# Turning the heads' outputs in 32x32 blocks on VectorE instead of transposing them on TensorE

## The chip, the core and the metric

The kernel runs on one core of one Trainium2 chip. The core has five engines, each with its own instruction queue: TensorE (PE, matrix products into PSUM), VectorE (DVE), ScalarE (ACT), GpSimd (POOL) and SyncE (SP, which here only issues DMA transfers); POOL and ACT issue DMA transfers too. Queues run in order and wait for each other by semaphores. The metric is the device time of one execution in microseconds (us).

## The reference: what is computed

One layer of a decoder trunk over 1024 tokens and 16 meta tokens ahead of them, 1024 channels, in float32. Two recurrent branches run side by side, each with four heads of 256 output channels: GLA and mLSTM. Each head's output is normalized over its 256 channels, scaled by a gain per channel, and multiplied by a gate; the branches are projected, merged and added, and a gated convolutional FFN follows.

```python
o_gla = from_chunks(head_rms(o_gla, gla_norm)) * silu(g_r)
o_ml  = from_chunks(head_rms(o_ml, ml_norm))   * sigmoid(m_o)
y = sigmoid(gate_a) * (o_gla @ w_branch_gla) + sigmoid(gate_b) * (o_ml @ w_branch_ml)
h = h + y @ w_out
def head_rms(y, g):
    return y * rsqrt(mean(y * y, axis=-1) + EPS) * g
```

The change concerns the way of a head's output from the recurrence, where tokens are rows, to the product with its gate, where channels are rows.

## The kernel before

**Stages.** The eight heads come first (s = 0 to 3 GLA, s = 4 to 7 mLSTM), then gates, branch products, merge and FFN. Matrix products that need float32 are done as three products of high and low parts. A scheduler places the instructions on each engine; the program's order is the default, and `tc.issue_after(x)` keeps a block behind the instruction x.

**Heads.** `main(gen)` steps through the dense projections (`value_proj`, `key_query_proj`, TensorE's bulk) and, at each step, lets one step of the recurrence of the head in work (`side`) and one of a finished head's epilogue (`closing`) in between. So head s is closed while head s+1 is scored and the projections for later heads run. In a GLA head, scores are made of `pk` tiles (decayed keys and queries, products on DVE and POOL, exponentials on ACT), TensorE's score products (`sc`, L862, PSUM tag "s"), and a masked copy into `A` (L879, DVE).

**The epilogue `post`.** A head's output lies in `oraw[0]` and `oraw[1]`, each 128 tokens x (4 chunks x 256 channels), and `om`, 2 rows that hold the last two meta tokens. ACT scales its rows by the reciprocal norm (L735, L736). Then, for each half j of the head's 256 channels: eight TensorE transposes of 128x128 (L744) turn the half to channels x tokens in two PSUM tiles `ot`; ACT copies each out into `of`, with the channel's gain as the scale (L746); a small transpose turns the meta rows (L757), which DVE copies out (L758); and one store by SP (L759) writes the 128 x 1026 half to the DRAM tile `osc`.

**Gates.** Gates are computed in pairs; the first eight pairs (q = 0 to 7) belong to the head halves, four pairs of GLA (`otdg`) and four of mLSTM (`otdm`). A pair's gates are computed by one Strassen-like scheme with four PSUM banks V, X, Y, Z per half of the tokens (`piece`), evicted by ACT and DVE (L1229 to L1245); weights are split on ACT and DVE (`gate_weights`, L1266 to L1293). `gate_finish(q - 1)` runs one pair behind: per gate it issues a load of the head half (`go`, two buffers "o0" and "o1") on POOL's queue (L1352), applies the gate's activation on ACT (L1353), multiplies on DVE into `go` (L1354), and stores the product from POOL's queue into `otd` (L1355). Loads stand in POOL's queue behind the stores of the pair before. The activated gates `gu` have two buffers of tag "u0", one of "u1", and for the last pairs every second one lies in "o1".

Of the kernel before, what the change touches and what calls it, by code (L numbers as in the profile page):

```python
# [9 lines left out]
F32 = mybir.dt.float32  # L10
# [7 lines left out]
P = 128  # L18
D = 1024
NM = 16  # L20
SEQ = 1024
# [24 lines left out]
def hybrid_kernel(ctx, tc, x, meta, norm_mix, w_in, b_in, gla_w_gate, gla_b_gate, gla_norm,  # L46
# [67 lines left out]
    with tc.issue_after(sent.ins):  # L114
        nc.scalar.activation(warm, one1, AF.Exp)

    rooted, flipped = [], {}

    def rstd_of(ss, n, w, pool, name):

# [384 lines left out]
    def cc(i):  # L505
        return col[:, i:i + 1]
# [28 lines left out]
            nc.vector.tensor_copy(lmask[b], mfs[:, P * (i + 1):P * (i + 2)])  # L535


    osc = {g: dram.tile([NK, P, NP], F32, name=f"osc{g}") for g in "gm"}
    gsc = {g: dram.tile([NK, P, NP], F32, name=f"gsc{g}") for g in "ab"}
    rsc = dram.tile([2, H, T], F32, name="rsc")  # L540
    msc = dram.tile([2 * H, T], F32, name="msc")
# [109 lines left out]
    def half_sums(t, m, c):  # L651
        for o, a, b in ((0, 1, 0), (1, 3, 1), (3, 3, 0), (2, 2, 3)):
            nc.gpsimd.tensor_tensor(t[:, o], t[:, a], t[:, b], OP.subtract)  # L653
        for i in range(2):
            nc.gpsimd.dma_start(tdn[i][m][:, :, 256 * c:256 * c + 256], t[:, 2 * i:2 * i + 2])
# [67 lines left out]
        yield  # L723


    def post(s, o, om, sc, ncols):

        h = s % 4
        g = "g" if s < 4 else "m"
        after = rooted[0]  # L730
        if 4 <= s < 7:
            with tc.issue_after(after.ins):
                after = token_sums(s - 3, nc.gpsimd)
        for c in range(NC):
            nc.scalar.activation(o(c), o(c), AF.Copy, scale=sc[:, c + 1:c + 2])  # L735
        nc.scalar.activation(om, om, AF.Copy, scale=sc[:2, 0:1])  # L736
        for _ in range(3 if s != 3 else 6):
            yield
        for j in range(2):
            of = hd.tile([P, T], F32, name=f"of{s}_{j}", tag="r", bufs=2)  # L740
            for gi in range(2):
                tp = ps.tile([P, 4, P], F32, name=f"ot{s}_{j}_{gi}", tag="s", bufs=3)
                for i in range(4):
                    nc.tensor.transpose(tp[:, i, :], o(4 * gi + i)[:, j * P:(j + 1) * P], ident)  # L744
                a, b = 2 + 512 * gi, 2 + 512 * (gi + 1)
                flipped[s] = nc.scalar.activation(of[:, a:b], tp.rearrange("p n w -> p (n w)"), AF.Copy,  # L746
                                                  scale=ncols[j]).ins
                if gi == 0:
                    yield
                    if 3 <= s < 7:  # L750
                        if j == 0:
                            with tc.issue_after(after.ins):
                                t = half_load(wp, "gst")
                        else:
                            half_sums(*t)
            tp = ps.tile([P, 4, P], F32, name=f"otm{s}_{j}", tag="s", bufs=3)
            nc.tensor.transpose(tp[:, 0, :2], om[:, j * P:(j + 1) * P], ident[:2, :2])  # L757
            nc.vector.tensor_scalar(of[:, 0:2], tp[:, 0, :2], ncols[j], None, OP.mult)  # L758
            nc.sync.dma_start(osc[g][2 * h + j], of[:, :NP])  # L759
            yield  # L760


# [46 lines left out]
    def gla(s):  # L809
# [74 lines left out]
        def level(b):  # L884


            if b == 1:
                p1 = raw.rearrange("p (n w) -> p n w", w=1)
                nc.scalar.activation(p1, lv(la[:, NM:], 1)[:, :, 1, :], AF.Exp, scale=1.0 / 16)
                nc.vector.tensor_tensor(p1, p1, lv(kv, 1)[:, :, 0, :], OP.mult)  # L890
                nc.vector.tensor_tensor(p1, p1, lv(qv, 1)[:, :, 1, :], OP.mult)
                return split_raw(f"pk{s}_1")
            pk = wtile(f"pk{s}_{b}")
            n = SEQ // (2 * b)
            pe, pl = (pk[:, 512 * i:512 * (i + 1)].rearrange("p (n w) -> p n w", w=b) for i in range(2))
            src = [lv(t, b)[:, :, 0, :] for t in (kv, bcv)]
            if b < 32:
                e = pk[:, :512].rearrange("p (i n h w) -> p i n h w", n=64 // b, h=2, w=b)
                pe = [e[:, :, :, 0, :], e[:, :, ::-1, 1, ::-1]]
                src = [[t.rearrange("p (i c n h w) -> p i c n h w", c=2, n=64 // b, h=2, w=b)[:, :, c, :, 0, :]  # L900
                        for c in range(2)] for t in (kv, bcv)]
            else:
                pe, src = [pe], [[t] for t in src]
            early = list(zip(pe, *src))
            b4 = lv(bcv, b)
            ref = b4[:, :, 0, b - 1:b].to_broadcast([P, n, b])
            for e, _, t in early:
                nc.vector.tensor_tensor(e, t[..., b - 1:b].to_broadcast(t.shape), t, OP.subtract)
            nc.vector.tensor_tensor(pl, b4[:, :, 1, :], ref, OP.subtract)
            with tc.issue_after(flipped[0]) if s == 1 and 0 in flipped else nullcontext():  # L910
                nc.scalar.activation(pk[:, :SEQ], pk[:, :SEQ], AF.Exp, scale=1.0 / 16)  # L911
            for eng, (e, k, _) in zip((nc.gpsimd, nc.vector), early):
                eng.tensor_tensor(e, e, k, OP.mult)  # L913
            nc.vector.tensor_tensor(pl, pl, lv(qv, b)[:, :, 1, :], OP.mult)
            return pk
# [117 lines left out]
        closing.append(post(s, o, om[:, :DV], sc, [cc(C_GN + j) for j in range(2)]))  # L1033


    above = []
# [1 line left out]
    def mlstm(s):  # L1038
# [119 lines left out]
        closing.append(post(s, o, om[:, :DV], sc, [cc(C_MN + 2 * h + j) for j in range(2)]))  # L1158


    def step(gens):
# [150 lines left out]
    def token_blocks():  # L1312
        for i in (0, 2, 1, 3):
            if i == 1:
                places()
            TB[i] = [gs.tile([P, 4, 514], F32R, name=f"T{p}{i}", tag=f"T{p}{i}") for p in "HL"]
        for p, c in enumerate((slice(0, W0), slice(W0, 514))):
            for i in (0, 2, 1, 3):
                nc.sync.dma_start(TB[i][1][:, :, c].bitcast(F32), tsc[p][i])
# [17 lines left out]
    def row(name, tag, bufs=1):  # L1337
        return gs.tile([P, T], F32, name=name, tag=tag, bufs=bufs)

    def places():  # L1340

        for i in range(2):
            go[0, i] = row(f"go0_{i}", f"o{i}")

    def gate_finish(q):
        for i, u in enumerate(gu.pop(q)):
            _, c, f, g, j = GATES[2 * q + i]
            if f is None:
# [3 lines left out]
            nc.gpsimd.dma_start(o[:, :NP], osc[g][j])  # L1352
            nc.scalar.activation(u[:, :NP], u[:, :NP], f, bias=cc(c))  # L1353
            nc.vector.tensor_tensor(o[:, :NP], u[:, :NP], o[:, :NP], OP.mult)  # L1354
            nc.gpsimd.dma_start(otd[g][j], o[:, :NP])  # L1355
# [779 lines left out]
```

## Time and profile before

| | |
|---|---|
| median of 3 runs | 1865.05 us (1864.66 to 1866.4) |
| profiled execution, from first to last instruction | 1865.1 us |
| TensorE's mean granted clock | 0.998 |
| busy: PE, DVE, ACT, POOL | 1846.0, 1227.9, 869.8, 427.5 us |
| transposes on TensorE (L744, L757) | 128 and 16, between 141 and 611 us of the span |
| gating products on DVE (L1354) | 16, between 661 and 803 us |

The profiled execution's own time is its span; it lies within the runs. The profile names instructions by line, engine, operation and tiles: `L744 PE MATMUL ot<-ident,or` is the transpose (a product with the identity) of a piece of `oraw` into `ot`. Durations of TensorE's instructions overlap, since matmuls are pipelined, so what one costs the queue is read from the distance between starts.

### The profile page before, as it was taken

The numbers are of one execution on the slowest core, as the hardware profiler recorded it, in microseconds if no ns is written. First come the engines' busy times: TensorE is split into PE (matmuls) and PEld (weight loads), VectorE is DVE, ScalarE is ACT, GpSimd is POOL, SyncE is SP. The second block draws the span as 40 slices with busy tenths as digits, with TensorE's granted clock in tenths as the row PEclk, the third lists the DMA queues.
The fourth block names the chain that finished last, engine by engine and source line by source line (L and its number), as shares of the span: only waits on it lengthen the run. The fifth ranks groups of instructions, "written<-read, shape, count | busy, mean of one in ns | idle before, by whom it ended". The sixth has DMA issues, their size and how long they took to land. (4 is left out here: it accounts for less than half of the span.)

```text
span 1865.1 us, 32629 instructions
## 1 busy us (share of the span) xinstructions
PE 1846.0 (99%) x13286; PEld 1768.5 (95%) x13286; DVE 1227.9 (66%) x1819; ACT 869.8 (47%) x1397; POOL 427.5 (23%) x485
## 2 busy tenths in 40 slices
PE   8999999999999999999999999999999999999998
PEld 7999999999999999999999999999999999977886
DVE  7966756655552566655523547798887887887876
ACT  6565564645544434322512335544434434465664
POOL 6310111205541001142381600012222222100100
PEclk9999999999999999999999999999999999999999
DMA  5211112144323655655963733333333333298894
GB/s 162 58 38 60 36 49 60 60 92 139 96 87 113 181 147 148 175 169 168 353 216 109 254 126 116 114 104 124 114 104 107 114 118 121 74 341 299 288 382 166
DMA packets 221820, 269.63 MB, mean 145 GB/s; under 512 B 13986, under 2 KB 177101, under 8 KB 221671
## 3 DMA queue, kind: packets, MB, share of 16 engines
q1 hardware_dynamic: 200447, 196.20, 34.0%
q0 software_dynamic: 18624, 62.62, 10.2%
q10 hardware_dynamic: 2600, 8.74, 1.3%
q8 instruction: 104, 1.70, 0.4%
q14 instruction: 45, 0.37, 0.1%
HBM read 197.91 MB, written 69.60 MB: 143 GB/s over the span
## 5 line engine op out<-in xcount | busy, mean ns | idle before, releaser
L653 POOL TENSOR_TENSOR ts<-ts 128x256 f32<-128x256 f32 x88 | 79.6, 911 | 47.0 <-DMA ts<-in_ffn_w_down_dram 44.9
L1654 POOL TENSOR_TENSOR SB<-SA,rg 128x512 f32<-128x512 f32 x20 | 32.4, 1622 | 240.2 <-issue 101.4
L276 PE MATMUL pv<-wH_mv,xH 128*128 128x256 f32 x256 | 74.8, 292 | 0.1
L276 PE MATMUL pv<-wH_gv,xH 128*128 128x256 f32 x256 | 74.5, 291 | 0.0
L1741 PE MATMUL po<-wH_wo,yH 128*128 128x256 f32 x256 | 72.5, 283 | 0.1
L276 PE MATMUL pv<-wH_gv,xL 128*128 128x256 f32 x256 | 72.0, 281 | 0.0
L276 PE MATMUL pv<-wL_mv,xH 128*128 128x256 f32 x256 | 71.9, 281 | 0.0
L1741 PE MATMUL po<-wL_wo,yH 128*128 128x256 f32 x256 | 71.7, 281 | 0.3 <-DVE wL_wo L147 0.3
L276 PE MATMUL pv<-wL_gv,xH 128*128 128x256 f32 x256 | 71.9, 281 | 0.0
L276 PE MATMUL pv<-wH_mv,xL 128*128 128x256 f32 x256 | 71.9, 281 | 0.0
L1741 PE MATMUL po<-wH_wo,yL 128*128 128x256 f32 x256 | 71.8, 281 | 0.0
L913 POOL TENSOR_TENSOR pk<-pk,kT 128x256 f32<-128x256 f32 (+1 forms) x24 | 29.6, 1237 | 182.7 <-ACT pk L911 165.1
L1689 DVE SCALAR_TENSOR_TENSOR cv<-u,fc,cv 128x1024 f32<-128x1024 f32 x44 | 65.1, 1482 | 0.4
L1636 POOL TENSOR_TENSOR A<-u2raw,A 128x512 fp32r<-128x512 f32 x20 | 42.4, 2122 | 86.3 <-ACT A L1635 86.3
L1447 PE MATMUL bg<-ogL,wH_bg 128*128 128x342 f32 x192 | 61.5, 320 | 0.0
L1447 PE MATMUL bg<-ogH,wH_bg 128*128 128x342 f32 x192 | 61.5, 320 | 0.0
L1447 PE MATMUL bm<-omH,wH_bm 128*128 128x342 f32 x192 | 61.4, 320 | 0.0
L1447 PE MATMUL bm<-omH,wL_bm 128*128 128x342 f32 x192 | 61.3, 319 | 0.0
L1447 PE MATMUL bg<-ogH,wL_bg 128*128 128x342 f32 x192 | 61.3, 319 | 0.0
L1447 PE MATMUL bm<-omL,wH_bm 128*128 128x342 f32 x192 | 61.2, 319 | 0.0
L280 DVE TENSOR_TENSOR v<-pv,bB 128x256 f32<-128x256 f32 x64 | 26.4, 417 | 39.5 <-PE pv L276 39.2
L1635 ACT ACTIVATE HA<-rg 128x1024 fp32r<-128x1024 f32 x16 | 17.0, 1060 | 73.0 <-PE Yu L1208 72.6
(821 smaller groups left out, 7511.3 us busy)
## 6 DMA issues: line engine op xcount, KB each, us to landing
gw<-in_w_in_dram SPq DMA_DIRECT2D x26, 512.0 KB, 5.7
ts<-in_ffn_w_down_dram POOLq DMA_DIRECT2D x44, 256.0 KB, 4.2
tdn<-ts POOLq DMA_DIRECT2D x44, 256.0 KB, 2.8
rg<-in_ffn_w_up_dram SPq DMA_DIRECT2D x22, 512.0 KB, 3.8
ru<-in_ffn_w_up_dram SPq DMA_DIRECT2D x22, 512.0 KB, 3.9
adr<-s SPq DMA_DIRECT2D x40, 256.0 KB, 2.8
rd<-in_ffn_w_down_dram SPq DMA_DIRECT2D x20, 512.0 KB, 11.2
do<-tdn SPq DMA_DIRECT2D x18, 512.0 KB, 6.0
```

Of the source, the lines that this page charges most:

```text
L276: nc.tensor.matmul(pt[:, :DV], a[:, k, t0:t0 + P], b[:, k % 4, :], start=(i == 0), stop=(i == 3 * NK - 1))
L280: nc.vector.tensor_tensor(vt[:n, c, :DV], pt[:n, :DV], bB[:n, :], OP.add)
L653: nc.gpsimd.tensor_tensor(t[:, o], t[:, a], t[:, b], OP.subtract)
L913: eng.tensor_tensor(e, e, k, OP.mult)
L1447: nc.tensor.matmul(pt[:, i, :n], a[:, k, :], b[k][:, base + t0:base + t0 + n], start=(k == 0 and j == 0), stop=(k == NK - 1 and j == 2))
L1635: nc.scalar.activation(h, src, AF.Copy)
L1636: eng.tensor_tensor(l, src, h.bitcast(F32), OP.subtract)
L1654: late.tensor_tensor(sb[:, 0:4], sa[:, 0:4], rg[:, 0:4], OP.subtract)
L1689: nc.vector.scalar_tensor_tensor(y, u[:, j:SEQ + j], fc[:, j, jj:jj + 1], y, OP.mult, OP.add)
L1741: nc.tensor.matmul(pt[:, :DV], a, b[:, k % 4, :], start=(k == 0 and i == 0), stop=(k == NK - 1 and i == len(terms) - 1))
```

## The change

`post` no longer uses TensorE. The meta rows are stored as they are to a DRAM tile `omd`. Per half of the tokens (j now counts halves of the tokens, `oraw[j]`) one DVE instruction turns 128x1024 in blocks of 32x32 (L745 in the new file): within each block, tokens and channels change places, and blocks are written in the order channel block, chunk. Four SP stores, one per 32 partitions, write 32 x 8 x 128 elements into `osc`, which now has 1024 columns, whose rows are channels and whose columns stand in the order (partition block a, chunk c, token j). ACT's evictions, the PSUM tiles `ot` and the ordering of one exponential behind the eviction (`flipped`) are gone.

The gating does the rest. `load_head(q, i)` loads the meta columns (128x2, from `omd` with rows and columns exchanged, L1340) and the 128x1024 main part (L1341) on POOL's queue into the only buffer left, "o0". The product becomes five scalar_tensor_tensor instructions on DVE, head x gain x gate, one for the meta columns (L1353) and four for the partition blocks (L1357), the gate read and written at the permuted places; the result stays in `gu` and is stored from there (L1358). The load of the pair's second head is issued after the first head's products, and that of the next pair's first head at the end of `gate_finish`. `gu` has two buffers of each kind.

```diff
@@ -535,7 +535,8 @@
-    osc = {g: dram.tile([NK, P, NP], F32, name=f"osc{g}") for g in "gm"}
+    osc = {g: dram.tile([NK, P, SEQ], F32, name=f"osc{g}") for g in "gm"}
+    omd = {g: dram.tile([H, 2, DV], F32, name=f"omd{g}") for g in "gm"}
     gsc = {g: dram.tile([NK, P, NP], F32, name=f"gsc{g}") for g in "ab"}
     rsc = dram.tile([2, H, T], F32, name="rsc")
     msc = dram.tile([2 * H, T], F32, name="msc")
@@ -723,7 +724,7 @@
         yield
 
 
-    def post(s, o, om, sc, ncols):
+    def post(s, oraw, om, sc):
 
         h = s % 4
         g = "g" if s < 4 else "m"
@@ -732,31 +733,27 @@
             with tc.issue_after(after.ins):
                 after = token_sums(s - 3, nc.gpsimd)
         for c in range(NC):
-            nc.scalar.activation(o(c), o(c), AF.Copy, scale=sc[:, c + 1:c + 2])
+            o = oraw[c // 4][:, DV * (c % 4):DV * (c % 4 + 1)]
+            nc.scalar.activation(o, o, AF.Copy, scale=sc[:, c + 1:c + 2])
         nc.scalar.activation(om, om, AF.Copy, scale=sc[:2, 0:1])
+        nc.sync.dma_start(omd[g][h], om)
         for _ in range(3 if s != 3 else 6):
             yield
+        dst = osc[g][2 * h:2 * h + 2].rearrange("t (q i) n -> i (t q) n", i=32)
         for j in range(2):
-            of = hd.tile([P, T], F32, name=f"of{s}_{j}", tag="r", bufs=2)
-            for gi in range(2):
-                tp = ps.tile([P, 4, P], F32, name=f"ot{s}_{j}_{gi}", tag="s", bufs=3)
-                for i in range(4):
-                    nc.tensor.transpose(tp[:, i, :], o(4 * gi + i)[:, j * P:(j + 1) * P], ident)
-                a, b = 2 + 512 * gi, 2 + 512 * (gi + 1)
-                flipped[s] = nc.scalar.activation(of[:, a:b], tp.rearrange("p n w -> p (n w)"), AF.Copy,
-                                                  scale=ncols[j]).ins
-                if gi == 0:
-                    yield
-                    if 3 <= s < 7:
-                        if j == 0:
-                            with tc.issue_after(after.ins):
-                                t = half_load(wp, "gst")
-                        else:
-                            half_sums(*t)
-            tp = ps.tile([P, 4, P], F32, name=f"otm{s}_{j}", tag="s", bufs=3)
-            nc.tensor.transpose(tp[:, 0, :2], om[:, j * P:(j + 1) * P], ident[:2, :2])
-            nc.vector.tensor_scalar(of[:, 0:2], tp[:, 0, :2], ncols[j], None, OP.mult)
-            nc.sync.dma_start(osc[g][2 * h + j], of[:, :NP])
+            t32 = hd.tile([P, T], F32, name=f"of{s}_{j}", tag="r", bufs=2)[:, :SEQ]
+            nc.vector.transpose(t32.rearrange("p (b c j) -> p c b j", b=8, c=4),
+                                oraw[j][:, :SEQ].rearrange("p (c b j) -> p c b j", c=4, b=8))
+            yield
+            if 3 <= s < 7:
+                if j == 0:
+                    with tc.issue_after(after.ins):
+                        t = half_load(wp, "gst")
+                else:
+                    half_sums(*t)
+            for a in range(4):
+                nc.sync.dma_start(dst[:, :, 256 * a + P * j:256 * a + P * j + P],
+                                  t32[32 * a:32 * a + 32].rearrange("p (b n) -> p b n", b=8))
             yield
 
 
@@ -907,8 +904,7 @@
             for e, _, t in early:
                 nc.vector.tensor_tensor(e, t[..., b - 1:b].to_broadcast(t.shape), t, OP.subtract)
             nc.vector.tensor_tensor(pl, b4[:, :, 1, :], ref, OP.subtract)
-            with tc.issue_after(flipped[0]) if s == 1 and 0 in flipped else nullcontext():
-                nc.scalar.activation(pk[:, :SEQ], pk[:, :SEQ], AF.Exp, scale=1.0 / 16)
+            nc.scalar.activation(pk[:, :SEQ], pk[:, :SEQ], AF.Exp, scale=1.0 / 16)
             for eng, (e, k, _) in zip((nc.gpsimd, nc.vector), early):
                 eng.tensor_tensor(e, e, k, OP.mult)
             nc.vector.tensor_tensor(pl, pl, lv(qv, b)[:, :, 1, :], OP.mult)
@@ -1312,7 +1308,7 @@
     def token_blocks():
         for i in (0, 2, 1, 3):
             if i == 1:
-                places()
+                load_head(0, 0)
             TB[i] = [gs.tile([P, 4, 514], F32R, name=f"T{p}{i}", tag=f"T{p}{i}") for p in "HL"]
         for p, c in enumerate((slice(0, W0), slice(W0, 514))):
             for i in (0, 2, 1, 3):
@@ -1337,10 +1333,12 @@
     def row(name, tag, bufs=1):
         return gs.tile([P, T], F32, name=name, tag=tag, bufs=bufs)
 
-    def places():
-
-        for i in range(2):
-            go[0, i] = row(f"go0_{i}", f"o{i}")
+    def load_head(q, i):
+
+        _, _, _, g, j = GATES[2 * q + i]
+        o = go[q, i] = row(f"go{q}_{i}", "o0")
+        nc.gpsimd.dma_start(o[:, :2], omd[g][j // 2][:, P * (j % 2):P * (j % 2) + P].rearrange("t d -> d t"))
+        nc.gpsimd.dma_start(o[:, 2:NP], osc[g][j])
 
     def gate_finish(q):
         for i, u in enumerate(gu.pop(q)):
@@ -1348,11 +1346,18 @@
             if f is None:
                 nc.scalar.dma_start(gsc[g][j], u[:, :NP])
                 continue
-            o = go[q, i] if q == 0 else row(f"go{q}_{i}", f"o{i}")
-            nc.gpsimd.dma_start(o[:, :NP], osc[g][j])
+            if i:
+                load_head(q, 1)
+            o, n = go[q, i], cc(C_GN + j % 2 if g == "g" else C_MN + j)
             nc.scalar.activation(u[:, :NP], u[:, :NP], f, bias=cc(c))
-            nc.vector.tensor_tensor(o[:, :NP], u[:, :NP], o[:, :NP], OP.mult)
-            nc.gpsimd.dma_start(otd[g][j], o[:, :NP])
+            nc.vector.scalar_tensor_tensor(u[:, :2], o[:, :2], n, u[:, :2], OP.mult, OP.mult)
+            for a in range(4):
+                ua = u[:, 2:NP].rearrange("p (c a j) -> p a c j", a=4, j=32)[:, a]
+                oa = o[:, 2:NP].rearrange("p (a c j) -> p a c j", a=4, j=32)[:, a]
+                nc.vector.scalar_tensor_tensor(ua, oa, n, ua, OP.mult, OP.mult)
+            nc.gpsimd.dma_start(otd[g][j], u[:, :NP])
+        if q + 1 < NK:
+            load_head(q + 1, 0)
 
     for tag in ("V1", "X1", "X0", "Y1", "V0", "Y0", "Z0", "Z1"):
         psG.tile([P, 512], F32, name=f"pg{tag}", tag=tag)
@@ -1371,7 +1376,7 @@
     u2 = wp.tile([P, T], F32, name="gu2", tag="gst", bufs=1)[:, :2 * W0].rearrange("p (a b) -> p a b", b=W0)
     behind_ = None
     for q in range(NG):
-        gu[q] = [row(f"gu0{q}", "u0", 2), row(f"gu1{q}", "o1" if q >= NK and q % 2 else "u1")]
+        gu[q] = [row(f"gu{i}{q}", f"u{i}", 2) for i in range(2)]
         for p in range(2):
             g = piece(psG, f"g{q}", p, gu[q], u2, WP[q], gate_block)
             next(g)
```

The calls of `post` pass `oraw` and no gain.

Where the instructions go, at three places. First DVE, while the scores of head 1 are made and head 0 is closed (`pk` are the decayed keys and queries, `pv` and `v` the value projection and its copy, `or` and `of` the head's output before and after the turn). Before:

```order
L913 TENSOR_TENSOR pk_4_1597<-pk_4_1597,kT_436 128x4x16x4
L914 TENSOR_TENSOR pk_4_1597<-pk_4_1597,qT_1299 128x512
L280 TENSOR_TENSOR v_1447<-pv_2_1528,bB_1445 128x256
L280 TENSOR_TENSOR v_1447<-pv_3_1571,bB_1445 128x256
L879 COPY_PREDICATED A<-mu_421,sc_1_1605 128x512
L908 TENSOR_TENSOR pk_8_1635<-bc_1288 128x32x8
L908 TENSOR_TENSOR pk_8_1635<-bc_1288 128x4x8x8
L909 TENSOR_TENSOR pk_8_1635<-bc_1288 128x512
L280 TENSOR_TENSOR v_1447<-pv_4_1609,bB_1445 128x256
```

and after:

```order
L909 TENSOR_TENSOR pk_4_1600<-pk_4_1600,kT_438 128x4x16x4
L910 TENSOR_TENSOR pk_4_1600<-pk_4_1600,qT_1301 128x512
L745 STREAM_TRANSPOSE of_0_1678<-or_0_1375 128x4x8x32
L280 TENSOR_TENSOR v_1449<-pv_2_1530,bB_1447 128x256
L905 TENSOR_TENSOR pk_8_1638<-bc_1290 128x32x8
L905 TENSOR_TENSOR pk_8_1638<-bc_1290 128x4x8x8
L906 TENSOR_TENSOR pk_8_1638<-bc_1290 128x512
L745 STREAM_TRANSPOSE of_1_1736<-or_1_1376 128x4x8x32
L280 TENSOR_TENSOR v_1449<-pv_3_1574,bB_1447 128x256
```

The two block transposes now stand among the score products of `pk`, and the copies of the value projection move behind them.

Second DVE again, in one round of the gates (`gw`, `gLSA`, `gLSB` are weights being split, `Yg`, `Zg`, `Xg` PSUM banks being evicted). Before:

```order
L1354 TENSOR_TENSOR go_0_7283<-gu_6970,go_0_7283 128x1026
L1269 TENSOR_TENSOR gA_7280<-gw_7066,gA_7280 128x512
L1354 TENSOR_TENSOR go_1_7288<-gu_6971,go_1_7288 128x1026
L1292 TENSOR_TENSOR gw_7293<-gw_7294,gw_7293 128x512
L1238 TENSOR_TENSOR gu_7199<-Yg_0_7202,gu_6543 128x256
L1230 TENSOR_TENSOR gu_7198<-Xg_1_7317,gu_7198 128x256
L1239 TENSOR_TENSOR gu_7199<-Zg_0_7203,gu_7199 128x256
```

and after, from the end of the first head's products to the second's:

```order
L1357 SCALAR_TENSOR_TENSOR gu_6817<-go_0_6919,col,gu_6817 128x8x32
L1235 TENSOR_TENSOR gu_7056<-Zg_0_7060,gu_7056 128x256
L1288 TENSOR_TENSOR gw_7160<-gw_7161,gw_7160 128x512
L1226 TENSOR_TENSOR gu_7055<-Xg_1_7184,gu_7055 128x256
L1265 TENSOR_TENSOR gLSA_7217<-gw_7161,gHSA_7216 128x512
L1265 TENSOR_TENSOR gLSA_7217<-gS_7213,gHSA_7216 128x512
L1289 TENSOR_TENSOR gw_7160<-gw_7160 128x512
L1353 SCALAR_TENSOR_TENSOR gu_6818<-go_1_7147,col,gu_6818 128x2
L1265 TENSOR_TENSOR gLSB_7249<-gw_7160,gHSB_7248 128x1024
L1240 TENSOR_TENSOR gu_7055<-Yg_0_7059,gu_6378 128x256
L1357 SCALAR_TENSOR_TENSOR gu_6818<-go_1_7147,col,gu_6818 128x8x32 x2
L1241 TENSOR_TENSOR gu_7056<-Zg_0_7060,gu_6378 128x258
```

The two heads' products, one instruction apart before, now stand seven instructions apart, with weight splits and evictions between and among them.

Third POOL's queue in the same stage. Before:

```order
L1352 DMA go_0_7055<-oscg 128x1026
L1352 DMA go_1_7060<-oscg 128x1026
L1355 DMA otdg<-go_0_7055 128x1026
L1355 DMA otdg<-go_1_7060 128x1026
L1352 DMA go_0_7283<-oscg 128x1026
```

and after:

```order
L1358 DMA otdg<-gu_6379 128x1026
L1340 DMA go_1_6671<-omdg 128x2x1
L1341 DMA go_1_6671<-oscg 128x1024
L1358 DMA otdg<-gu_6380 128x1026
L1340 DMA go_0_6681<-omdg 128x2x1
L1341 DMA go_0_6681<-oscg 128x1024
```

Two loads followed by two stores have become a store, a small load and a load in turn.

More of the change, by code (lines that the diff above doesn't have):

```diff
@@ L115, in hybrid_kernel @@
         nc.scalar.activation(warm, one1, AF.Exp)
-    rooted, flipped = [], {}
+    rooted = []
     def rstd_of(ss, n, w, pool, name):
@@ L1032, in gla @@
         sc = rstd_of(ss, DV, NC + 1, hd, f"rs{s}")
-        closing.append(post(s, o, om[:, :DV], sc, [cc(C_GN + j) for j in range(2)]))
+        closing.append(post(s, oraw, om[:, :DV], sc))
     above = []
@@ L1157, in mlstm @@
         nc.vector.tensor_tensor(sc, sc, rc, OP.mult)
-        closing.append(post(s, o, om[:, :DV], sc, [cc(C_MN + 2 * h + j) for j in range(2)]))
+        closing.append(post(s, oraw, om[:, :DV], sc))
     def step(gens):
```

## Prediction

> **What bounds the kernel now.** I read the page's busy times and slices first, then TensorE's list of waits (line waited for, releaser, total us, times, longest).
>
> ```profile
> span 1865.1 us, 32629 instructions
> PE 1846.0 (99%) x13286; PEld 1768.5 (95%) x13286; DVE 1227.9 (66%) x1819; ACT 869.8 (47%) x1397; POOL 427.5 (23%) x485
> PE   8999999999999999999999999999999999999998
> DVE  7966756655552566655523547798887887887876
> PE xtp L425 <- DVE xt L417: 2.3, 4, 0.7
> ...
> PE sct L852 <- DVE A L879: 0.4, 1, 0.4
> ```
>
> TensorE is busy in every slice; its longest entry of waits is 2.3 us in all, and the one for a GLA head's scores is 0.4. So what leaves TensorE's queue shortens the program by the spacing that it held there, as long as no new wait enters. DVE is at 66%, but the change gives it work in two places, and those are read apart below. The span is 0.05 us above the median of the runs (1865.05), so the sum is made against 1865.1 and stands for the median too.
>
> **The change, part by part.**
>
> *1. The transposes leave TensorE:* 128 large ones (eight per half, two halves, eight heads) and 16 small ones for the meta tokens.
>
> ```profile
> L744 PE MATMUL ot<-ident,or x128: 270/272/328, 141.4 to 610.2; 128*128 128x128 f32 x128
> L757 PE MATMUL otm<-ident,om x16: 217/218/219, 146.1 to 610.4; 2*128 2x2 f32 x16
> 141.42 0.60 PE L744 MATMUL ot<-ident,or 128*128 128x128 f32 x4
> 141.85 1.06 PE L862 MATMUL sc<-pk 128*128 128x128 f32 x8
> ...
> 609.27 0.32 PE L234 MATMUL pj<-xH,wL_gb 128*128 128x342 f32 x1
> 609.43 1.04 PE L744 MATMUL ot<-ident,or 128*128 128x128 f32 x8
> 610.39 0.22 PE L757 MATMUL otm<-ident,om 2*128 2x2 f32 x1
> 610.54 0.43 PE L234 MATMUL pc<-xH,wH_gb 128*128 128x342 f32 x1
> 610.81 0.32 PE L234 MATMUL pc<-xL,wH_gb 128*128 128x342 f32 x1
> ```
>
> The durations overlap in the pipeline (a timeline row's first column is its start), so I price by starts. Four transposes hold the queue for 141.85 − 141.42 = 0.43, eight for 610.39 − 609.43 = 0.96, a meta one for 610.54 − 610.39 = 0.15. A half costs 0.96 + 0.15 = 1.11, a head 2.22, eight heads 17.8. Behind the group the first projection matmul holds 0.27 (610.54 to 610.81) where the one at 609.27 held 0.16: 0.11 lost where transposes cut into a run of projections. Ten such cuts is my estimate, among 16 halves of which those in the GLA heads lie beside other small matmuls: 1.1. Together 18.9 go.
>
> The Trainium skill, page "TensorE: Matmul & The Clock Gate", section "Part 4: PE-mode transpose", gives about 275 ns for a 128x128 transpose inside a kernel. The durations in the rows (272) agree, the starts (0.11 to 0.12 apart) do not; by the page 128 x 0.275 = 35 would go, and the time be about 1830, which is nearly rival D below.
>
> *2. The evictions leave ACT and DVE.*
>
> ```profile
> L746 ACT ACTIVATE of<-ot,col 128x512 f32<-128x512 f32 x32 | 21.6, 682 | 15.3 <-PE ot L744 15.2
> L758 DVE TENSOR_SCALAR of<-otm,col 128x2 f32<-128x2 f32 x16 | 3.4, 215 | 20.1 <-PE otm L757 20.1
> ```
>
> ACT, at 47%, loses 21.6 us, and DVE 3.4. On the path I count zero, since TensorE waits for neither. A gain is possible, because PSUM banks of tag "s" come free for the scores and ACT's queue is shorter ahead of their exponentials: up to 3 or 4 us, the size of TensorE's few waits on these engines, so the range's lower end lies that far below the sum.
>
> *3. Sixteen block transposes enter DVE,* two per head, 128x1024 each, among the next head's score products. No such instruction stands in this trace. The nearest rows are a plain pass over 128x1026, 1.219 us, and a masked copy of 128x512, at the longest 1.328, so 2.65 for 1024.
>
> ```profile
> L1354 DVE TENSOR_TENSOR go<-gu,go 128x1026 f32<-128x1026 f32 x16 | 19.5, 1219 | 0.0
> L879 DVE COPY_PREDICATED A<-mu,sc x20: 682/730/1328, 74.1 to 301.1; 128x512 f32<-128x512 uint8 x20
> 128.00:162.00 34.00, 34.00 (x269) 32.90 (x268) 29.46 (x51) 18.18 (x28) 7.72 (x6) 1.00 0.17 54
> 200.00:236.00 36.00, 36.00 (x277) 34.88 (x276) 28.87 (x50) 19.14 (x33) 8.77 (x8) 1.00 0.18 51
> 274.00:312.00 38.00, 37.64 (x283) 36.42 (x282) 31.10 (x50) 20.92 (x37) 8.69 (x11) 1.00 0.19 60
> ```
>
> The last three rows (window; us; busy PE, PEld, DVE, ACT, POOL; granted clock, DMA share, GB/s) are the stretches in which a GLA head is closed while the next is scored. DVE has 34.0 − 29.5 = 4.5, 36.0 − 28.9 = 7.1 and 38.0 − 31.1 = 6.9 us to spare. I take 1.2 a transpose, the plain pass, since this too reads and writes every element once. Then 2.4 enter a head, 0.4 leaves (two of L758), and TensorE arrives 2.2 sooner: 4.2 of the first stretch's 4.5. It fits, but barely, and the next head's decay products queue behind the transposes on DVE, and TensorE's score matmuls behind those: I charge 0.5 for short waits, and 0.4 for one more like the wait for A above. At 2.65 the demand is 5.3 − 0.4 + 2.2 = 7.1 against 4.5, 7.1 and 6.9: 2.6 + 0 + 0.2 = 2.8; if each of the six is fully exposed by what it exceeds the plain pass, 6 x 1.43 = 8.6. In the other heads the slices show DVE at half or less: zero.
>
> The Trainium skill, page "VectorE: DVE Perf Modes", section "The three transpose paths", puts 311 ns to a 128x128 bf16 transpose on VectorE; eight of them would be 2.5 us. No transpose on DVE is in this trace; by the page rival C would be the case.
>
> *4. The stores.* A head issues nine on SP (meta rows, then four per half) instead of two, in runs of 512 bytes instead of 4104.
>
> ```profile
> L759 SPq DMA_DIRECT2D oscm<-of x8: 319/338/339, 449.0 to 612.1; - x8
> SPq L759 <- DVE of L758: 162.2, 15, 35.2
> oscg<-of SPq DMA_DIRECT2D x8, 513.0 KB, 6.4
> ```
>
> Seven more at 0.338 are 2.4 us a head, 19 in all, while SP stood for 162 waiting at the old stores. What queues behind them are weight loads; the old stores landed in 6.4. DMA is at 0.17 to 0.19 of its time in those stretches. Zero on the path; without that cover a weight load would come 2.4 later.
>
> *5. The norm gain moves into the gating.* Per gated head a product over 128x1026 becomes one of 128x2 and four of 128x256 with a gain.
>
> ```profile
> L1019 DVE SCALAR_TENSOR_TENSOR S<-S,dl,up 128x256 f32<-128x256 f32 x28 | 13.3, 476 | 25.0 <-PE up L985 23.6 <-PE op L1024 0.8
> 680.00:700.00 20.00, 20.00 (x170) 20.00 (x169) 12.72 (x23) 7.54 (x13) 2.16 (x4) 1.00 0.58 158
> ```
>
> 4 x 0.476 + 0.215 = 2.12 against 1.22, 0.9 more a head and 1.8 a round of 20 us. DVE is idle for 7.3 of those: zero.
>
> *6. One buffer for the loaded heads.* Here a new wait can enter.
>
> ```profile
> 680.31 1.22 DVE L1354 TENSOR_TENSOR go<-gu,go 128x1026 f32<-128x1026 f32 x1
> 681.82 0.54 POOL L1355 DMA_DIRECT2D otdg<-go  x1 [8.32 <-DVE go L1354]
> 683.56 0.54 POOL L1355 DMA_DIRECT2D otdg<-go  x1 [1.20 <-DVE go L1354]
> 687.06 0.54 POOL L1352 DMA_DIRECT2D go<-oscg  x1 [2.96 <-DMA otdg<-go]
> 691.23 0.55 POOL L1352 DMA_DIRECT2D go<-oscg  x1 [3.63 <-DMA otdg<-go]
> DMA to landing us min/median/max: 4.0/4.9/7.2
> ...
> DMA to landing us min/median/max: 4.7/5.8/8.9
> L647 POOL DMA_DIRECT2D ts<-in_ffn_w_down_dram x44: 704/728/830, 354.7 to 1059.9; - x44
> ```
>
> (The landing lines: of the old loads, then of the old stores to otdg.) Before, both heads lie ready when their gates are done. Now head (q,1) is loaded only when head (q,0)'s products have read the buffer, and (q+1,0) after those of (q,1). Call leg L the time from the issue of a store, over the meta load and the main load behind it, to that load's landing. A round is two legs and about 5.0 (two times 2.1 of products and the handover), so the loop takes TensorE's place at 2L + 5.0 = 20.0, L = 7.5. The meta load is new: 256 runs of four bytes; POOL takes 0.73 to issue a load of 256 runs. Low end of L: 0.54 + 0.73 + 4.9 = 6.2. High end: 0.54 + 0.73, and the load lands only as late as the latest store, 8.9: 10.2. I take 7.2, the low end plus 1.0 for the store of equal size beside it, nearest the load's own row: the old load of 687.06 ran beside the store of 683.56 too. The old products of 680.31 were followed by a store at 681.82; with 0.9 more of products and the work that stands between them the store of (q,0) goes out at some 683.1, and the next head lies there at 690.3.
>
> ```profile
> 689.02 0.42 DVE L1244 TENSOR_TENSOR gu<-Yg,gu 128x256 f32<-128x256 f32 x1
> 689.10 0.28 PE L1208 MATMUL Xg<-TH,gHSB 128*128 128x256 f32 x1
> 694.81 0.28 PE L1208 MATMUL Zg<-TH,gHSA 128*128 128x258 f32 x1
> ```
>
> What a late head holds up on DVE are such evictions of the gates' PSUM banks. TensorE leaves bank Z at 689.10 and wants it again at 694.81: with 2.1 of products ahead of the eviction, 694.8 − 2.1 − 0.4 = 692.3 is the latest landing, 2.0 of slack. I charge 1 for the first and the uneven rounds. A gain is excluded, since TensorE does not wait in this stretch (20.0 of 20.0).
>
> The Trainium skill, page "DMA: Bandwidth & Descriptors", section "Rules for kernel authors", says that a last dimension that is not contiguous becomes one descriptor per element, which speaks against the meta load. No load of four-byte elements stands in this trace, so it neither agrees nor differs; if those descriptors hold up the main load, rival B is the case.
>
> Sum: 1865.1 − 18.9 + 0.5 + 0.4 + 1 = **1848**.
>
> **Rivals.**
>
> *B: the gate loop takes TensorE's place.* Each of seven rounds grows by 2L − 15, less the 2.0 of slack once. L = 8.5 gives 7 x 2 − 2 = 12 and 1847 + 12 = 1859; L = 9.5 gives 26 and 1873, slower than before. It decides where it eats the 18 of gain: 2L − 15 = (18 + 2) / 7 = 2.9, L = 8.9. For it: stores took up to 8.9, and an old load waited 3.63 for one; against it, the loads' 4.9.
>
> *C: DVE late in three GLA heads.* A transpose of 2.65 gives 2.8 to 8.6 more: 1850 to 1857, middle 1853. For it: 4.5 us of room in the first stretch; against it, transposes are no copies under a mask.
>
> *D: the full durations are freed.* 128 x 0.272 + 16 x 0.217 = 38.3, so 1827. The starts speak against it.
>
> *E: the 18.9 come back* as waits on engines that TensorE's pace now covers, about 1865. TensorE's list of waits, where no entry is over 2.3, speaks against it: such waits would have to come up in many places at once.
>
> **How the numbers follow.** A measurement of this kernel tells 0.2% (3.7 us) from nothing. The predicted case, 1844 to 1851: 0.62. C: 0.14. B up to 1861: 0.08; 1861 to 1869: 0.05; beyond 1869, slower: 0.05. E: 0.04. D: 0.02. Faster: 0.62 + 0.14 + 0.08 + 0.02 = 0.86; same 0.05 + 0.04 = 0.09; slower 0.05. The range 1844 to 1861 leaves out D, E and B's upper part, 0.16.
>
> **What would show it.** Right: TensorE busy 18 to 19 less and still at 99%; transposes of 1.2; no gate-stage wait of TensorE over 2 us; main loads landing some 5 to 6 after issue. Wrong: in the gate stage DVE idle on a load, TensorE on PSUM, rounds over 20 (B); transposes of 2 or more with TensorE waiting for pk or A (C); starts closing up by 0.27 a transpose (D); waits elsewhere that sum to over 10 (E).

## The result and the profile after

The changed kernel takes 1854.08 us (median of 4 runs, 1853.46 to 1857.03) against 1865.47 (1864.66 to 1866.4) for the kernel before: ratio 0.994, interval 0.9929 to 0.9952. It is faster by 11.4 us, where 17 were forecast; 1854.1 lies inside the range of 1844 to 1861, but outside its predicted case of 1844 to 1851. The profiled spans differ by 12.9 us (1865.1 and 1852.2).

The page's first lines, TensorE's list of waits (releaser, total us, times, longest), and the group and source rows of the new DVE instructions, all of the changed kernel:

```profile
span 1852.2 us, 32513 instructions
PE 1826.6 (99%) x13142; PEld 1751.7 (95%) x13142; DVE 1247.4 (67%) x1883; ACT 850.6 (46%) x1365; POOL 439.2 (24%) x501
...
PE sct L849 <- DVE A L876: 1.9, 2, 1.4
PE pv L276 <- DVE v L280: 1.5, 1, 1.5
PE bg L1452 <- DVE ogL L1436: 1.4, 2, 0.8
PE pj L234 <- DVE v L280: 1.1, 1, 1.1
PE bg L1452 <- ACT ogH L1435: 0.7, 1, 0.7
...
L745 DVE STREAM_TRANSPOSE of<-or x16: 1197/1245/1247, 133.3 to 581.6; 128x1024 f32<-128x1024 f32 x16
its engine sat idle before it (us, times) until:
  ACT or L737: 6.1, 7
```

TensorE is busy 19.4 us less (1846.0 to 1826.6), about as forecast (18.9). But the span fell by only 12.9: five entries that were absent or 0.4 before now stand in the list of waits, 6.6 us in all. A block transpose takes 1.245, close to the 1.2 taken; what the forecast did not have is the last row: DVE, whose queue runs in order, stood 6.1 us in seven places until ACT had scaled the rows that the transpose reads.

Where the difference arises can be read by comparing the start of each TensorE matmul with the start of the same matmul before. Each head should give what the two halves held; four of them (1, 4, 5, 7) give 2.44 to 2.46, which is taken as all of it:

| stretch | head 0 | 1 | 2 | 3 | 4 | 5 | 6 | 7 | gates | start of branch products | FFN |
|---|---|---|---|---|---|---|---|---|---|---|---|
| after minus before, us | −1.62 | −2.46 | −1.24 | −1.01 | −2.46 | −2.45 | −0.90 | −2.44 | +0.4 | +2.9 | −2.1 |

So 14.6 of 8 x 2.45 = 19.6 came out of the heads; 5.0 were lost in heads 0, 2, 3 and 6, and 2.9 more where the branch products begin. The FFN's part is not the change's: its code is the same in all runs, and in the traces of the other runs it moved by −0.3 to −3.5 us. In the kernel before, TensorE waits 1.7 and 0.5 us in its down projection and then has a granted clock of 0.50 for 3.4 us (the number behind the five engines' busy times), which the trace after does not show; some 1.5 of the 2.1 arise there:

```profile
1642.70:1646.10 3.40, 3.40 (x10) 2.62 (x9) 3.40 (x4) 3.40 (x4) 0.00 (x0) 0.50 1.03 411
```

(The stretches sum to −13.4; the other 0.5 to the spans' 12.9 lies outside them.)

### The profile page after: what moved, and what is told of

It is laid out like the page before. It is cut to its first block, busy times and chain, and to the rows that moved or that the text cites. A ratio compares the mean times of both kernels' runs of the same rounds, so it can differ in the third digit from the quotient of the medians.

```text
span 1852.2 us, 32513 instructions
## 1 busy us (share of the span) xinstructions
PE 1826.6 (99%) x13142; PEld 1751.7 (95%) x13142; DVE 1247.4 (67%) x1883; ACT 850.6 (46%) x1365; POOL 439.2 (24%) x501
## 4 chain that ended last, share of the span: by engine, by line
PE 82%; DVE 7%; DMA 4%; issue 3%; POOL 2%; ACT 2%; SPq 0%; POOLq 0%; DVEq 0%; ACTq 0%
PE pj L234 9%; PE Yu L1204 7%; PE Zu L1204 7%; PE Xu L1204 6%; PE pv L276 5%; PE bm L1452 5%; PE bg L1452 5%; PE Zg L1204 4%; PE Yg L1204 4%; PE Xg L1204 4%; PE po L1746 4%; PE Vu L1204 3%; PE pdX L1903 2%; PE pdZ L1903 2%; PE pdY L1903 2%
## 5 line engine op out<-in xcount | busy, mean ns | idle before, releaser
L2001 POOL TENSOR_TENSOR fr<-fv,mhalf 128x1 f32<-128x1 f32 x8 | 12.2, 1528 | 165.1 <-DVE fv L1994 94.3
L276 PEld LDWEIGHTS pv<-wH_mv,xH 128*128 128x128 f32 x256 | 48.2, 188 | 2.6 <-DVE v L280 2.3
```

What stands on the lines that cost most here:

```text
L276: nc.tensor.matmul(pt[:, :DV], a[:, k, t0:t0 + P], b[:, k % 4, :], start=(i == 0), stop=(i == 3 * NK - 1))
L2001: rooted[:] = [nc.gpsimd.tensor_tensor(rs, v, mhalf, OP.pow)]
```

## The experiments

**The lost 2.9: where the rows lie.** The first eight loads of the gated GLA rows, POOL's timeline of the kernel before and of the changed one (the bracket is idle time and what ended it):

```profile
889.47 2.09 POOL L1429 DMA_DIRECT2D ogL<-otdg  x4 [3.35 <-PE Yg L1208]
894.09 2.09 POOL L1429 DMA_DIRECT2D ogL<-otdg  x4 [2.53 <-PE Zg L1208]
```

```profile
879.69 4.17 POOL L1434 DMA_DIRECT2D ogL<-otdg  x8 [8.06 <-PE Zg L1204]
```

Before, four loads go as soon as the product ahead of the last has read its operands, and four after the last. Now all eight wait for the last: the memory of the first tile is another. The change took "o1" away and gave "u1" a second buffer, which is as much memory, but at another place. Run e1 reserves that place where "o1" was:

```diff
                 load_head(0, 0)
+                row("gu1p", "o1")
...
-        gu[q] = [row(f"gu{i}{q}", f"u{i}", 2) for i in range(2)]
+        gu[q] = [row(f"gu0{q}", "u0", 2), row(f"gu1{q}", ("u1", "o1")[q % 2])]
```

> The changed kernel, with the second buffer of the odd gate rows placed where the second head buffer (o1) was before; everything else as changed. Places theory: the first four loads of the branch products wait only for TensorE's last-but-one product again, are issued some 4 us before the other four, and TensorE's waits for ogL and ogH (2.1 us, with 2.9 lost on its clock of the program) go: about 1851 against 1854.1. Rival: the loads are late because the last heads' stores are late; then nothing changes, 1854.

1851.39 us (1850.48 to 1851.97), ratio to before 0.9918 (0.9903 to 0.9933). POOL's rows of e1, and the branch products' source rows before, after and in e1 (the last pair of numbers is the first and the last start):

```profile
876.71 2.10 POOL L1435 DMA_DIRECT2D ogL<-otdg  x4 [4.72 <-DVE wL_bg L147]
879.98 2.08 POOL L1435 DMA_DIRECT2D ogL<-otdg  x4 [1.18 <-PE Zg L1204]
```

```profile
L1447 PE MATMUL bg<-ogH,wH_bg x192: 313/319/337, 904.7 to 995.1; 128*128 128x342 f32 x192
```

```profile
L1452 PE MATMUL bg<-ogH,wH_bg x192: 314/320/425, 891.4 to 983.8; 128*128 128x342 f32 x192
```

```profile
L1453 PE MATMUL bg<-ogH,wH_bg x192: 314/320/338, 890.8 to 981.2; 128*128 128x342 f32 x192
```

The changed kernel's 13.3 us of lead at the first product (904.7 − 891.4) are 11.3 at the last (995.1 − 983.8); in e1 13.9 stay 13.9, and no wait for ogL or ogH is left. The places theory holds in the time and the starts; the release was forecast as TensorE's last-but-one product, while the bracket of the first four loads names DVE's split `wL_bg`, and they go 3.3 us ahead of the others. The 0.4 of the gates is gone in e1 too (0.0). Both once more on one chip, five rounds each:

> The changed kernel once more, beside the next run on one chip: 1854, ratio 0.994, as in the first timing; TensorE's waits for ogL and ogH at the start of the branch products sum to 2.1 us again.

> The kernel with the restored places once more, on the same chip as the changed one: 2.7 us less than it (places theory), 1851.4, ratio 0.992. If the first difference was the chip's, the two agree within 1 us.

1855.63 (1851.51 to 1855.84, ratio 0.994, 0.9927 to 0.9954) against 1851.83 (1849.65 to 1852.19, ratio 0.9923, 0.9911 to 0.9936). The medians differ by 3.8, the profiled spans by 4.4. Of the 4.4, 2.3 arise around the start of the branch products (1.3 of it waits for ogL and ogH), 0.7 in the FFN, and 1.5 in the first 16 us, ahead of all that was changed. So single traces differ by more than a microsecond at the start, and losses are read from the steps inside a stretch.

**The lost 5.0 in the heads.** Two theories at first: the transposes on DVE's queue, or the nine stores. Run e2 leaves the transposes out and stores the rows as they are:

```diff
-            t32 = hd.tile([P, T], F32, name=f"of{s}_{j}", tag="r", bufs=2)[:, :SEQ]
-            nc.vector.transpose(...)
+            t32 = oraw[j][:, :SEQ]
```

> The changed kernel without the sixteen block transposes; the rows are stored unturned, all else stays. VectorE-queue theory: the 5.0 us that heads 0, 2, 3 and 6 failed to give come back, 19.6 are gained by the end of the heads instead of 14.6, about 1849. Stores theory (nine stores of 512-byte runs, SP behind them): they stay lost, 1854.

Its four runs took 1850.72 (the profiled one) and 1854.56 to 1854.76; the 4 us between them are not explained, so the starts decide. Head 0 gives 0.8 more than in the changed kernel and head 6 1.1 more; heads 2 and 3 give no more than they did, and by the end of the heads 1.3 of the 5.0 are back (other heads lose a few tenths: the rows' buffers are now held until they are stored). Both theories fall short. DVE in the stretch in which head 2 is closed, changed kernel, then e2 (busy PE, PEld, DVE, ACT, POOL):

```profile
272.00:299.00 27.00, 25.63 (x199) 24.78 (x199) 25.83 (x42) 13.09 (x20) 7.36 (x7) 1.00 0.25 64
```

```profile
272.00:299.00 27.00, 25.43 (x199) 24.59 (x198) 24.90 (x40) 13.49 (x23) 7.54 (x7) 1.00 0.28 67
...
PE sct L847 <- DVE A L874: 1.6, 1, 1.6
```

Without a single transpose DVE is busy 24.9 of 27 us there and TensorE waits 1.6 for A. So DVE's list is nearly full in the scores, and TensorE, 2.45 earlier per head, has caught up with it. Yet in head 1's closing DVE is almost as full in the changed kernel, and nothing is lost there:

```profile
201.00:228.00 27.00, 27.00 (x215) 26.43 (x214) 25.35 (x42) 12.67 (x20) 7.58 (x6) 1.00 0.16 40
```

Is it then the amount of work, or its order? Run e3 keeps the work and moves each transpose behind a later copy of the value projection, after four more steps of the epilogue (`anchor[0]` is the newest such copy):

```diff
-        for _ in range(3 if s != 3 else 6):
+        for _ in range(7 if s != 3 else 10):
...
+            with tc.issue_after(anchor[0]):
                 nc.vector.transpose(...)
```

> The changed kernel with each block transpose held behind a later copy of the value projection, so that on VectorE it stands behind the next head's score copies and no longer waits for ScalarE's scaling; the work is the same. Position theory: the loss in the heads falls from 5.0 to 1 or less, about 1850. Capacity theory (VectorE simply has too little room in those heads): the loss stays 4 to 5, 1854.

1863.26 us (1860.67 to 1866.76), ratio 0.9982 (0.9972 to 0.9992): nearly all of the gain is gone. The transposes no longer wait, yet against the changed kernel head 0 loses 3.2 net (a 0.8 gain, then 4.0), head 2 2.6 and head 7 6.3. In head 0 they now stand ahead of `kq`, which the next scores need; in head 7 the epilogue's later steps moved POOL's work too, and DVE waited there 5.76 for POOL's root, which is no finding on the transposes. Part of these losses is not waiting: four times TensorE's granted clock falls to one half for 3.4 us behind waits, beside heads 0, 2 and 7 and at the branch products. The first three:

```profile
161.20:164.60 3.40, 3.40 (x16) 3.40 (x14) 3.14 (x6) 2.15 (x5) 0.00 (x0) 0.50 1.09 319
301.20:304.60 3.40, 2.94 (x6) 1.91 (x7) 3.40 (x5) 0.60 (x1) 0.00 (x0) 0.50 0.77 201
594.70:598.10 3.40, 3.04 (x11) 3.04 (x12) 1.23 (x1) 1.94 (x4) 0.00 (x0) 0.50 0.67 223
```

TensorE is busy 12.8 us in the four, so by an estimate they cost up to 6.4 us. The traces of the changed kernel, e1, e5, e10, e11 and e12 have no such stretch between their first 20 and their last 6 us. Run e5, on e1, moves only two: head 0's first, and head 6's.

```diff
+            with tc.issue_after(leveled[0]) if s == 0 and j == 0 else tc.issue_after(anchor[0]) if s == 6 else nullcontext():
                 nc.vector.transpose(...)
```

> The kernel with the restored places (1851.4), and two of the heads' block transposes moved on VectorE: head 0's first behind the decay products of level 16, so that it no longer waits 2.1 us for ScalarE's scaling, and head 6's each behind one more copy of the value projection, for which TensorE waited 1.5. Queue-position theory: 0.8 us in head 0 and 1.1 in head 6 come back, about 1849.5. Capacity theory for head 0: TensorE waits there still, only head 6's 1.1 come back, about 1850.3.

1852.58 (1851.85 to 1854.67), not better than e1. Both forecast gains appear at their places (0.81 in head 0, 1.13 in head 6), and both are lost again within some 25 us (2.2 and 1.9). TensorE's and DVE's timeline of e5 show how, in head 0:

```profile
159.75 0.51 PE L833 MATMUL sc<-kq,ones 128*128 128x512 f32 x1 [1.96 <-DVE kq L827]
...
156.75 1.22 DVE L147 TENSOR_TENSOR wL_gq<-wr_gq,wH_gq 128x1024 fp32r<-128x1024 f32 x1
157.88 1.22 DVE L147 TENSOR_TENSOR wL_gv<-wr_gv,wH_gv 128x1024 fp32r<-128x1024 f32 x1
159.01 0.69 DVE L827 TENSOR_TENSOR kq<-An,kq 128x512 fp32r<-128x512 f32 x1
```

TensorE stands 1.96 us for `kq`, and directly ahead of it in DVE's queue are two weight splits, 1.22 each, that TensorE needs later. Two tries at taking work off DVE followed. Run e6 gives two weight splits in head 2's stretch and three small-row operations beside head 3 to POOL:

```diff
-    parted = []
+    parted, RELIEF = [], ("mq0", "mv0_0")
...
-        parted[:] = [nc.vector.tensor_tensor(wL, raw, wH.bitcast(F32), OP.subtract).ins]
+        eng = nc.gpsimd if name in RELIEF else nc.vector
+        parted[:] = [eng.tensor_tensor(wL, raw, wH.bitcast(F32), OP.subtract).ins]
```

> The kernel with the restored places (1851.4), with VectorE relieved in the two full stretches: the weight splits that stand among head 2's last score copies (two of 1.2 us) and three of the small-row operations beside head 3 (4.4 us) go to GpSimd; the transposes stay where they are. Capacity theory: head 2's loss of 1.2 and head 3's of 1.45 shrink to some 0.3 each, about 1849.5. Rival (the loss there comes from the stores or from ScalarE): nothing comes back, 1851.4. GpSimd being slower and its results late would show as new waits on it.

1861.24 (1858.51 to 1861.71): a loss of 10, in heads 2 (2.9) and 3 (1.7 gained, then 7.5 lost). TensorE waits 5.6 for one copy of the value projection and 3.2 for A, and its clock is at one half for 3.4 and 6.8 us behind these waits. Ahead of that copy DVE stood 4.4 us for a small-row result of POOL. It says nothing on capacity. Run e8 takes the same splits off DVE without POOL, and two row copies:

```diff
+        if name in ("mq0", "mv0_0"):
+            parted[:] = [nc.scalar.activation(wL, raw, AF.Copy).ins]
...
-        nc.vector.tensor_copy(st[0:4], a)
+        nc.scalar.activation(st[0:4], a, AF.Copy)
```

> The kernel with the restored places (1851.4), with two of the four weight splits of the first mLSTM head's query and value left out on VectorE (ScalarE writes a plain copy, of 1.06 us, instead of the remainder, so those low parts are not what the reference needs), and two row copies beside head 3 (0.7 and 1.1 us) on ScalarE too. VectorE's list in the scores of head 3 is 2.4 us shorter, beside head 3's closing 1.8 shorter; nothing goes to GpSimd. Capacity theory: the wait for A in head 2's closing (1.4) goes and 1.2 come back there, and about 1 beside head 3: 1849. Rival (stores or ScalarE set that pace): no change or a loss, 1851 and more.

One run, 1853.29. In head 2 what was forecast: 1.10 come back, and TensorE's wait of 1.37 for A is 0.25:

```profile
294.78 1.12 PE L852 MATMUL sct<-A,flip 128*128 128x512 f32 x2 [0.25 <-DVE A L879]
```

Beside head 3 it lost 2.4: the row copy on ACT stands behind the head's scaling, a table load of 1.28 us and another row operation, DVE stands 2.3 us for it, and TensorE 2.05 behind both. The row copies alone:

> The kernel with the restored places and only the two row copies on ScalarE; the computation is complete. Capacity theory: about 1 us comes back beside head 3, 1850.4. Rival: 1851.4 or more; a wait of TensorE for the copies of the value projection of 1 us and more stays.

1853.66 (1851.49 to 1854.17), the same 2.4 lost beside head 3: a miss. Of the 2.4, 0.9 is lost when TensorE's wait of 2.06 us ends (1.32 in e1); the rest is lost behind it at half the clock, where projection matmuls start 0.29 us apart instead of 0.16:

```profile
359.92 0.53 PE L234 MATMUL pj<-xH,wH_mk 128*128 128x348 f32 x1 [2.06 <-DVE v L280]
360.10:363.50 3.40, 3.40 (x13) 3.40 (x14) 3.27 (x6) 1.50 (x2) 0.00 (x0) 0.50 0.23 50
```

So the last run does not change the work at all. It is e1 with head 0's first transpose moved as in e5, and with the score copies and `kq` (its split into high and low part included) given a priority above the weight splits:

```diff
-            return nc.vector.copy_predicated(dst, m, ...)
+            with hp(4000):
+                return nc.vector.copy_predicated(dst, m, ...)
...
-        kq.append(diagonal(1))
+        with hp(4000):
+            kq.append(diagonal(1))
```

> The kernel with the restored places (1851.4 and 1851.8 so far), head 0's first transpose behind the level-16 decay products as in e5, and now the score copies and the diagonal products (kq) of the GLA heads given a higher priority than the weight splits, so that on VectorE kq of head 1 stands ahead of two splits of 1.2 us that it stood behind in e5. List-order theory (what TensorE waits for must stand early in VectorE's list, the sum of the work matters less): head 0 gives its full 2.45, 0.8 comes back, and e5's wait of 2.0 for kq is gone: 1850.6. Capacity theory: the wait comes back elsewhere in the same head (kh, the weight splits), 1851.5 to 1853.

1849.29 us (1848.81 to 1851.14), ratio 0.9913 (0.99 to 0.9927), the lowest median of all, though its interval overlaps that of e1 (0.9903 to 0.9933), so the starts carry the reading. DVE's timeline at the place shown of e5, and two entries of TensorE's list of waits:

```profile
154.27 1.00 DVE L828 TENSOR_TENSOR kq<-An,kq 128x512 fp32r<-128x512 f32 x1
155.19 0.68 DVE L915 TENSOR_TENSOR pk<-pk,qT 128x512 f32<-128x512 f32 x1
155.80 1.21 DVE L147 TENSOR_TENSOR wL_gq<-wr_gq,wH_gq 128x1024 fp32r<-128x1024 f32 x1
...
PE pv L278 <- DVE v L282: 1.5, 1, 1.5
PE pj L234 <- DVE v L282: 1.3, 1, 1.3
```

`kq` ends before the splits, the wait for it is gone and head 0 keeps its 0.8; head 2 gives 1.0 more, and no wait for A is in the list. DVE is busy as long as in e1 (1251.4 and 1250.1 us). List order, at the same amount of work, is enough to give back what heads 0 and 2 lost, head 2 but for 0.2. The two waits that remain are those of heads 6 and 3.

**The price of a transpose.** Run e7 is the kernel before with each transpose twice.

```diff
                     nc.tensor.transpose(tp[:, i, :], ..., ident)
+                    nc.tensor.transpose(tp[:, i, :], ..., ident)
```

> The kernel before with each of TensorE's transposes issued twice; nothing else is changed. By starts (0.43 for four, 0.15 for a meta one): 17.8 us more, less what falls into waits, so 1882 to 1884. By full durations: 38 us, 1904. The extra work also gives the other engines time, so a little less than 17.8 is no surprise.

One run, 1878.84, below the forecast of 1882. By the end of the heads TensorE is 14.2 us later: 0.44 for each four, and 0.5 with a meta transpose, so 1.9 a head. Taken out, a head's transposes gave 2.45; the 0.6 between is put down here to breaking into the other products, which no run shows by itself. (After the heads, 3.5 us vanish in the FFN.)

**The gate loop.** Run e4 lengthens the leg by four more meta loads.

```diff
+        for m in range(4):
+            nc.gpsimd.dma_start(o[:, NP + 2 * m:NP + 2 * m + 2], omd[g]...)
         nc.gpsimd.dma_start(o[:, 2:NP], osc[g][j])
```

> The changed kernel with four more meta loads ahead of each main load of the gating (into unused columns), which adds 4 x 0.72 = 2.9 us to a leg measured at 6.2: L = 9.1. By the prediction's formula a round grows by 2 x 9.1 - 15 = 3.2 us, seven times, less 2: 20 us, 1874. If the loop has more room than 2L + 5.0 says, less; if it has none of the room (TensorE always just covered), 7 x 2 x 2.9 = 41 us.

One run, 1877.98, 24 more than the changed kernel where 20 were forecast. TensorE now waits for gate banks (17.4 us in four entries), and in two stretches of 3.4 us its granted clock is 0.50, which by an estimate takes up to 3.4 us of the 24:

```profile
PE Xg L1204 <- DVE gu L1226: 6.4, 6, 1.4
PE Zg L1204 <- DVE gu L1241: 5.8, 6, 2.8
...
696.20:699.60 3.40, 3.40 (x18) 3.40 (x18) 3.40 (x8) 0.01 (x1) 0.00 (x0) 0.50 0.29 88
709.80:713.20 3.40, 3.40 (x18) 3.40 (x17) 2.64 (x7) 0.18 (x1) 0.56 (x1) 0.51 0.02 5
```

Rival B's formula is borne out to a fifth at this one length of leg. Its threshold, L = 7.5, was not located by a run; by it the changed kernel, at 6.2, has 1.3 us of leg to spare.

## Why the prediction was right, and where it was off

- **Step 1 (transposes)**: 18.9 forecast; 19.6 measured, where four heads of 2.45 stand for all eight. Pricing by starts was right; rival D, and the Trainium skill's 275 ns in "TensorE: Matmul & The Clock Gate", "Part 4: PE-mode transpose", would have given nearly twice that (e7: 0.11 each, back to back). That the sum came so close is in part luck: the transposes alone cost 1.9 a head in e7 where 2.22 were priced, and the cuts into other products, charged with 0.14 a head, must then stand for some 0.6.
- **Step 3 (block transposes)** is the term that was mis-sized. 0.9 was charged (0.5 and 0.4); 5.0 were lost. The price of an instruction was right (1.245 against 1.2; the rule of the Trainium skill's "VectorE: DVE Perf Modes", "The three transpose paths", 311 ns for 128x128 in bf16, would have made it 2.5). Two things failed. The spare time was taken from windows and slices that were too wide: for head 2, 6.9 us were read over 38 us, where the scores themselves left 4.4 of 28; for head 3, zero was set by "DVE at half or less", where its slice of 47 us shows 6 tenths and the 14 us of its closing were full before the change. The kernel before:

```profile
276.00:304.00 28.00, 27.64 (x216) 26.62 (x215) 23.60 (x40) 14.48 (x24) 7.62 (x7) 1.00 0.20 56
356.00:370.00 14.00, 13.98 (x104) 13.57 (x102) 13.70 (x18) 8.61 (x13) 7.05 (x7) 1.00 0.36 117
```

  And the queue was taken as a sum, though it is a list: the transposes and the weight splits stand ahead of what TensorE wants next, and the transposes wait themselves for ACT's scaling. In heads 0 and 2 this was the larger failure, since e12 gives 1.8 us back with the work unchanged. Rival C had the place in heads 0 and 2, but its price was per transpose and would not have found heads 3 and 6, the former a GLA head closed beside mLSTM work, the latter an mLSTM head. The measured 1854.1 lies in C's band (1850 to 1857), but C's reason, transposes of 2.65, did not come true; that the range held is luck to this extent.
- **Step 6 (gates)**: 1 charged, 0.4 measured (0.0 in e1, e11 and e12, so the 0.4 goes with the places). L was taken as 7.2; it was 6.2 (0.54 + 0.71 + 4.9), its low end. The Trainium skill's rule in "DMA: Bandwidth & Descriptors", "Rules for kernel authors", on one descriptor per element, did not hold up the main load here:

```profile
L1340 POOL DMA_DIRECT2D go<-omdg x8: 715/715/768, 578.0 to 709.6; - x8
...
DMA to landing us min/median/max: 2.4/4.3/6.0
```

  The meta load lands in 4.3 us, and the main load behind it in 4.9 as before. One sign that the prediction named for rival B did appear: DVE stood idle for loads, most of it for the meta load (the rows of its product, L1353), while TensorE's list has no wait in the gates:

```profile
  DMA go<-omdm: 11.0, 5
  DMA go<-omdg: 8.8, 4
```

- **Missing**: the 2.9 us at the branch products. The change swaps two buffers of equal size, and the prediction looked at their number, not at what is later put in their place (e1).
- **Steps 2, 4 and 5** were zero on the path, as far as the starts show: no wait for the stores' queue, and DVE's extra work in the gates (14.12 of 20 us busy) is hidden.

So the gain of 17 became 11.4: 0.7 more from step 1, 4.1 less from step 3 (5.0 where 0.9 was charged), 0.6 more from step 6 and 2.9 less from the places make 11.3.

What stays open: how to free heads 3 and 6, which still lose 1.5 each in the best version. In both, TensorE waits for a copy of the value projection that stands behind long operations in DVE's queue. In head 6 a transpose is among them, and without it, in e2, 1.1 came back; moving it gave and took (e5). In head 3 the cause is not shown: e2 gave nothing back, and no run takes away the nine stores, so they are not ruled out there.

## What to carry to other kernels

Work moved from a bound engine to an idle one is priced by the list that it enters: look at the stretch between two things that the bound engine waits for, at the length of those few microseconds, and ask which instructions stand ahead of each. An instruction that waits (here for ACT) blocks all behind it, and a prefetch that stands ahead (the weight splits) can cost more than a move gains (2.2 against 0.8 in head 0 of e5). A wait can cost more than its length, when the granted clock falls behind it (0.9 of waiting and 1.5 of slower matmuls in e9). When a change adds or drops a buffer, see what takes its place in memory later, even two stages on.

## What was not expected of the hardware

- The granted clock fell to one half in the middle of the program, always for 3.4 us or twice that, in six traces between their first 20 and last 6 us: before (once), e3 (four times), e4 (twice), e6 (three), e8 (two) and e9 (once). In the 3.4 us ahead of each fall TensorE had stood idle for 1.5 (e8) to 3.4 us (e3). Idle time of 1.5 to 1.9 us in such a stretch was not always followed by a fall (1.75 in e10 was not), more than 1.9 always was. In e5 a wait of 1.96 us had no such effect; the clock changes only at multiples of 3.41 us from its first record, and cut there the wait falls into pieces of 0.86 and 1.09.
- Taken out, a head's transposes gave TensorE 0.6 us more than the same transposes cost when issued a second time, back to back (2.45 against 1.9).
